# Differential-attention core scored two units ahead, stage loads issued earlier, and some copies moved to ScalarE

## Chip, cores and metric

The kernel runs on one core of a Trainium2 chip (trn2). The metric is device time in microseconds (us) of one execution, median of three runs. Engines: TensorE (PE, with its weight loads as PEld), VectorE (DVE), ScalarE (ACT), GpSimd (POOL); SyncE (SP) issues nearly all DMAs.

## What is computed

One encoder layer over 1024 positions of width 1024. One normalised input is projected into three branches (mLSTM, differential attention, retention) and three gates; the gated branch outputs are summed, projected, normed and added to x; a SwiGLU feed-forward follows. The part that matters most here:

```python
# 8 heads, 2 components of 64 per head, values of 128
for blk in range(S // Q_BLOCK):                  # 8 blocks of 128 queries
    kend = q0 + Q_BLOCK
    s = einsum('bqhcd,bkhcd->bhcqk', qb, kb)     # two score maps per head
    s = where(allowed, s - slope * dist, -inf)
    p = softmax(s, axis=-1)
    a = p[:, :, 0] - lam * p[:, :, 1]
    outs.append(einsum('bhqk,bkhe->bqhe', a, vb))
...
y = gm * (hm @ w_mlstm_out) + gd * (hd @ w_diff_out) + gr * (hr @ w_ret_out)
x = x + rmsnorm(y @ w_out);  x = x + rmsnorm((silu(a) * u) @ w_ffn_out)
```

## The kernel before, in words

Matmuls of full precision are made of three passes on a high and a low part of each operand (`mm3`, L111 to L113); `split_sbuf` (L105 on ACT, L106 on DVE) makes the two parts. The large products (input projection, feed-forward) use seven products in place of eight (`Seven`, `Unit`, `steady`); a unit has seven steps of 12 matmuls, and `follow` runs one step between two `yield`s.

Stages in order of time: `turned` transposes the normed x into seven operand roles (`L255` transposes, then ACT L265 makes the high part, DVE L266 a plain copy, DVE L267 the low part); `projections` runs the units while the mLSTM and retention cores are woven in; then `diff_core`, the differential attention; then the rest of the merge and `w_out` blocks with `norm_steps`; then `turned` again for the feed-forward; `feed_forward`; `down`.

`diff_core` runs 64 units (8 heads, and per head query blocks qb = 7 down to 0). Of a unit, `scores` makes two score maps (PE L850), adds the distance bias and takes the row maximum (DVE L852), negates it (L856) and takes the exponential with its row sum (ACT L857). `weights` combines the two maps (DVE L863, L865, L866). `turn` transposes the result (PE L876) and copies it (ACT or DVE L878). `values` multiplies with v (PE L886) and norms (ACT L213, DVE L890 and L207, POOL L208, DVE L894). `finish` transposes the output (PE L904). In the loop, while unit n is worked on, the scores of unit n+1 are issued after `turn` of n, and its `weights` in the second half.

`weave` runs other work between: each value that the core yields, times a rate, gives the number of steps of `dense` (the merge products of the mLSTM and retention branches, 12 matmuls a step, operands `bh`, `bl`, `wh`, `wl`) that are issued there. Tiles come from pools of fixed size: `big` (tag T, 32 tiles of 4 KB per partition), `half_tile` (tag s2k, 14 tiles of 2 KB), PSUM with 4 banks for dense work and 4 for the rest. A list scheduler then settles the order on each engine, and each engine and DMA queue runs its own list strictly in order.

In `diff_core` the loads of head 0 (`diff_load`, L809 and L810, `diff_load_v`, L814) are issued when the core starts. In `down`, `operands` loads one block of the hidden activations (L1230) and splits it just ahead of its products.

Of the kernel before, what the change touches and what calls it, by code (L numbers as in the profile page):

```python
# [8 lines left out]
F32 = mybir.dt.float32  # L9
# [3 lines left out]
ALU = mybir.AluOpType  # L13
# [27 lines left out]
def trunk(ctx: ExitStack, tc: tile.TileContext, x, norm_gains, w_in, mlstm_conv, mlstm_gate_bias,  # L41
# [18 lines left out]
    def big(shape, dtype=F32, name="t"):  # L60
        return pool.tile(shape, dtype, tag="T", bufs=N_T, name=nm(name))
# [187 lines left out]
    def turned(src, sh, g, seven, xs):  # L249


        for kt in range(KT) if sh == 0 else (4, 5, 0, 1, 6, 7, 2, 3):
            ps = psum()
            for i in range(4):
                nc.tensor.transpose(ps[:, i * P:(i + 1) * P], src[i][:, kt * P:(kt + 1) * P], ident)  # L255
            col = pcol[:, g + kt:g + kt + 1]
            role, q = "A" + str(sh + 1) + str(kt // 4 + 1), kt % 4
            if (role, q // 2) not in xs:
                xs[role, q // 2] = big([P, 2, HALF], name="hx")
            x = xs[role, q // 2][:, q % 2, :]  # L260
            if role == "A21":
                nc.scalar.activation(x, ps, AF.Copy, scale=col)
            else:
                h, l = seven.slot(role, q)
                nc.scalar.activation(h, ps, AF.Copy, scale=col)  # L265
                nc.vector.tensor_scalar(x, ps, col, None, op0=ALU.mult)  # L266
                nc.vector.tensor_sub(l, x, h.bitcast(F32))  # L267
            yield

    def left_sums(seven, xs):  # L270
# [548 lines left out]
        return slice((c % 4) * P, (c % 4 + 1) * P)  # L819

    def diff_core():
        ndist = big([P, S], name="ndist")
        nc.scalar.dma_start(ndist, c_dist)
        for sh in (1, 0):
            diff_load(0, sh, diff_qk[0])
        diff_load_v(0, diff_qk[0])

        def scores(u):
            hd, qb = u["hd"], u["qb"]
            d = diff_qk[hd]  # L830
            if qb < 4 and hd + 1 < DH:
                after = diff_qk[hd + 1]
                if qb == 3:
                    diff_load(hd + 1, 1, after)
                    diff_load_v(hd + 1, after)
                if qb == 1:
                    diff_load(hd + 1, 0, after)
# [70 lines left out]

        units = [dict(hd=hd, qb=qb) for hd in range(DH) for qb in reversed(range(NT))]
        scores(units[0])  # L910
        yield 6
        weights(units[0])
        for n, u in enumerate(units):
            after = units[n + 1] if n + 1 < len(units) else None
            turn(u)
            if after is not None:
                scores(after)
            if n > 0:
                finish(units[n - 1])
# [5 lines left out]
            if u["qb"] == 0:  # L925
                diff_qk[u["hd"]].clear()
            yield w
        finish(units[-1])

# [126 lines left out]
    def norm_steps(sh, i):  # L1056

        st = sh * 4 + i
        t = z[sh][i]
        xt = big([P, D], name="xr")  # L1060
        nc.sync.dma_start(xt, x[st * P:(st + 1) * P, :])
        rstd = norm_factor(t)
        yield
        nc.vector.scalar_tensor_tensor(t, t, rstd, gains[1], op0=ALU.mult, op1=ALU.mult)
        nc.vector.tensor_add(xt, xt, t)  # L1065
        nc.sync.dma_start(x2_dram[st * P:(st + 1) * P, :], xt)
        rstd = norm_factor(xt)
        yield
        nc.vector.tensor_scalar(t, xt, rstd, None, op0=ALU.mult)

    def out_blocks():
        acc = {}
# [112 lines left out]
        keep("S4", p, s[3])  # L1185
        first.h = second.h = None

    def feed_forward():
        keep_hidden(*ups[:2])
        for n, _ in enumerate(steady(ups[3:])):  # L1190
            if n % 14 == 6:
                keep_hidden(*ups[n // 7 + 2:n // 7 + 4])
        for r in ROLES:
            h2.drop(r)

    def down():


        gains[3] = gain(3)
        f = [None] * NT  # L1200
        w = []

# [22 lines left out]
            nc.vector.tensor_sub(b12, b21, b12)  # L1225
            return b12

        def operands(role_l, role_r, p):
            t = half_tile()
            nc.sync.dma_start(t, hid[role_l][p])  # L1230
            o = [parts_tile([P, HALF]) for _ in range(2)]
            split_sbuf(*o[0], t)
            split_sbuf(*o[1], right(role_r, p))
# [5 lines left out]
        def product(role_l, role_r, ps, more):  # L1239
            for p in range(NP):  # L1240
                if role_r == "B11":
                    load(p)
                o = operands(role_l, role_r, p)
                for j in range(4):
                    step(ps[j], o, j, p == 0, p == NP - 1, more)

# [15 lines left out]
        def x2_of(st):  # L1262
            xt = big([P, D], name="x2")
            nc.sync.dma_start(xt, x2_dram[st * P:(st + 1) * P, :])
            return xt

        f[:] = [big([P, D], name="f") for _ in range(NT)]
        px = [psum(True) for _ in range(4)]
        product("A11", "B11", px, False)
# [3 lines left out]
        product("S1", "T1", py, False)  # L1273
        for j in range(4):
            nc.scalar.copy(f[j + 4][:, halfs(1)], py[j])
        product("S2", "T2", px, True)
        for j in range(4):
            nc.scalar.copy(f[j][:, halfs(1)], px[j])
        product("S4", "B22", py, True)
        for j in range(4):  # L1280
            nc.vector.tensor_add(f[j][:, halfs(1)], py[j], f[j][:, halfs(1)])
        product("S3", "T3", px, True)
# [3 lines left out]
        product("A12", "B21", pz, False)  # L1286
        for j in range(4):
            nc.vector.tensor_add(f[j][:, halfs(0)], pz[j], f[j][:, halfs(0)])
        s2 = [small([P, 2], "s2", bufs=8) for _ in range(NT)]
        held = []  # L1290
        for p in range(NP):
            o = operands("A22", "T4", p)
# [50 lines left out]
    ups = [up(i, own=i == 2) for i in range(FB)]  # L1343
    units[2].own = True
    made = [0]

    def projections():

# [97 lines left out]
    feed_forward()  # L1446
    down()


# [48 lines left out]
```

## Time and profile before

| | |
|---|---|
| median of three runs | 2746.5 us (2746.33 to 2747.31) |
| profiled execution | 2744.93 us, of which the span 2743.1 us |
| PE busy | 2563.2 us (93%) |
| DVE busy | 1755.2 us (64%) |
| ACT busy | 1222.5 us (45%) |
| mean granted TensorE clock | 0.971 |

The span is the time from the first to the last instruction in the trace. Busy PE time is made of matmuls that overlap in a pipeline, so a busy PE may still run below its best pace; the granted clock says how fast it was allowed to run (1.00 is 2.4 GHz).

### The profile page before, as it was taken

Reading aid. Unit: us, or ns where it says so; the run is one execution under the profiler, and the core shown is the slowest. Engines: PE = TensorE matmul, PEld = TensorE weight load, DVE = VectorE, ACT = ScalarE, POOL = GpSimd, SP = SyncE. Lnnn points to the kernel's source line nnn. Section 1 sums busy time; section 2 is a strip of 40 time slices with the busy share of each in tenths; the row PEclk is TensorE's granted clock in tenths of the full one; section 3 lists DMA queues with packets and bytes.
Section 4 is the critical chain, followed back from the end, with each engine's and each line's share of the span. In section 5 each row is a group of like instructions: output and inputs, shape, how many; then the busy total and the mean of one; then the engine's idle time right before and its main releaser. Section 6 shows DMA issues by size and latency. Waiting matters only on the chain. (4 is left out here: it accounts for less than half of the span.)

```text
span 2743.1 us, 35302 instructions
## 1 busy us (share of the span) xinstructions
PE 2563.2 (93%) x12061; PEld 2083.4 (76%) x12061; DVE 1755.2 (64%) x3638; ACT 1222.5 (45%) x2480; POOL 262.5 (10%) x393
## 2 busy tenths in 40 slices
PE   6999999999999999999978869879998999998997
PEld 4778888888788888888766657667876888886885
DVE  7678877666666666565456666664368555654756
ACT  4554554454344444554434444442254333332544
POOL 3000000000000000000000001112123201110000
PEclk9999999999999999999989989989998999999999
DMA  3244445444545555443564456546433323337342
GB/s 118 87 134 123 138 123 155 132 139 124 153 127 158 160 151 159 131 130 101 160 165 117 131 143 175 147 131 207 146 108 96 122 86 111 101 99 266 104 135 87
DMA packets 402079, 368.93 MB, mean 134 GB/s; under 512 B 18957, under 2 KB 302046, under 8 KB 401898
## 3 DMA queue, kind: packets, MB, share of 16 engines
q1 hardware_dynamic: 399424, 364.45, 44.5%
q10 hardware_dynamic: 2474, 2.22, 0.3%
q8 instruction: 95, 1.56, 0.2%
q14 instruction: 86, 0.70, 0.1%
HBM read 249.92 MB, written 116.69 MB: 134 GB/s over the span
## 5 line engine op out<-in xcount | busy, mean ns | idle before, releaser
L105 ACT CAST wh<-ws 128x512 fp32r<-128x512 f32 (+1 forms) x622 | 385.0, 623 | 748.2 <-PE ps L112 546.0
L106 DVE TENSOR_TENSOR wl<-ws,wh 128x512 fp32r<-128x512 f32 (+1 forms) x622 | 454.4, 734 | 234.3 <-ACT wh L105 228.9
L302 DVE TENSOR_TENSOR ws<-ws,ws 128x512 f32<-128x512 f32 x216 | 148.8, 689 | 99.8 <-DMA ws<-in_w_in_dram 56.1
L111 PE MATMUL ps<-bh,wh 128*128 128x512 f32 x384 | 156.9, 416 | 9.9 <-ACT bh L105 6.5
L112 PE MATMUL ps<-bl,wh 128*128 128x512 f32 x384 | 155.5, 407 | 1.7 <-DVE bl L106 1.7
L113 PE MATMUL ps<-bh,wl 128*128 128x512 f32 x384 | 155.1, 406 | 0.0
L315 ACT COPY s2k<-ps 128x512 f32<-128x512 f32 x234 | 136.0, 582 | 17.8 <-PE ps L113 15.7
L111 PE MATMUL ps<-A11h,wh 128*128 128x512 f32 x312 | 127.8, 410 | 11.4 <-ACT wh L105 9.1
L111 PE MATMUL ps<-S1h,wh 128*128 128x512 f32 x312 | 127.1, 409 | 8.1 <-ACT S1h L105 7.5
L857 ACT ACTIVATE sb<-sb,nmx 128x896 f32<-128x896 f32 (+7 forms) x128 | 98.3, 769 | 69.6 <-DVE nmx L856 69.4
L111 PE MATMUL ps<-S2h,wh 128*128 128x512 f32 x312 | 125.8, 404 | 3.6 <-ACT s2k L315 3.6
L111 PE MATMUL ps<-wh,wh 128*128 128x512 f32 x308 | 118.3, 392 | 11.4 <-ACT wh L105 11.4
L113 PE MATMUL ps<-A11h,wl 128*128 128x512 f32 x312 | 125.9, 403 | 2.3 <-DVE wl L106 2.3
L112 PE MATMUL ps<-S1l,wh 128*128 128x512 f32 x312 | 125.7, 403 | 1.5 <-DVE S1l L106 1.5
L111 PE MATMUL ps<-S3h,wh 128*128 128x512 f32 x312 | 125.0, 401 | 0.7 <-ACT s2k L315 0.7
L112 PE MATMUL ps<-A11l,wh 128*128 128x512 f32 x312 | 125.6, 403 | 0.0
L111 PE MATMUL ps<-S4h,wh 128*128 128x512 f32 x312 | 125.5, 402 | 0.0
L113 PE MATMUL ps<-S1h,wl 128*128 128x512 f32 x312 | 125.2, 401 | 0.0
L112 PE MATMUL ps<-wl,wh 128*128 128x512 f32 x308 | 120.9, 393 | 4.3 <-DVE wl L106 4.3
L111 PE MATMUL ps<-A12h,wh 128*128 128x512 f32 x312 | 124.7, 400 | 0.1
L112 PE MATMUL ps<-S2l,wh 128*128 128x512 f32 x312 | 124.5, 400 | 0.1
L111 PE MATMUL ps<-A22h,wh 128*128 128x512 f32 x312 | 124.6, 399 | 0.0
(294 smaller groups left out, 6520.3 us busy)
## 6 DMA issues: line engine op xcount, KB each, us to landing
ws<-in_w_in_dram SPq DMA_DIRECT2D x112, 512.0 KB, 4.5
ws<-in_w_ffn_in_dram SPq DMA_DIRECT2D x44, 512.0 KB, 3.9
m_dram<-s2k SPq DMA_DIRECT2D x64, 256.0 KB, 2.1
ch<-m_dram SPq DMA_DIRECT2D x32, 512.0 KB, 6.0
r_dram<-s2k SPq DMA_DIRECT2D x64, 256.0 KB, 2.3
ch<-r_dram SPq DMA_DIRECT2D x32, 512.0 KB, 5.2
qk_dram<-s2k SPq DMA_DIRECT2D x64, 256.0 KB, 3.3
dk<-qk_dram SPq DMA_DIRECT2D x64, 256.0 KB, 5.1
```

Of the source, the lines that this page charges most:

```text
L105: nc.scalar.copy(hi, src)
L106: nc.vector.tensor_sub(lo, src, hi.bitcast(F32))
L111: nc.tensor.matmul(ps, lh, rh, start=start, stop=False, skip_group_check=more)
L112: nc.tensor.matmul(ps, lh, rl, start=False, stop=False, skip_group_check=more)
L113: nc.tensor.matmul(ps, ll, rh, start=False, stop=stop, skip_group_check=more)
L302: self.eng.tensor_tensor(*sub[r], op=ALU.subtract)
L315: nc.scalar.copy(t, ps)
L857: nc.scalar.activation(sb[c], sb[c], AF.Exp, bias=nmx, scale=slope, accum_out=sm[:, c:c + 1])
```

## The change

Six edits. (1) In `turned`, for odd tiles, the low part is made straight from PSUM by one DVE operation, and the plain copy is made on ACT. (2) `diff_core` scores unit n+2 while unit n is worked on; the first two units are scored ahead with a larger yield, and score tiles of at most 512 columns come from the s2k pool. (3) The loads of the next head are issued at qb 4 and 3, those of head 0 in the last part of `projections`. (4) The last scaling in `norm_steps` goes from DVE to ACT. (5) `down` becomes a generator: its first loads and its first split are issued inside the last unit of `feed_forward`, and it keeps up to three hidden blocks loaded ahead. (6) The weave rate of the core is 63/892 instead of 64/832.

```diff
@@ turned
-                nc.vector.tensor_scalar(x, ps, col, None, op0=ALU.mult)
-                nc.vector.tensor_sub(l, x, h.bitcast(F32))
+                if kt % 2:
+                    nc.vector.scalar_tensor_tensor(l, ps, col, h.bitcast(F32), op0=ALU.mult, op1=ALU.subtract)
+                    nc.scalar.activation(x, ps, AF.Copy, scale=col)
+                else:
+                    nc.vector.tensor_scalar(x, ps, col, None, op0=ALU.mult)
+                    nc.vector.tensor_sub(l, x, h.bitcast(F32))
@@ diff_core
-            sb = u["sb"] = [big([P, kend], name="sb") for _ in range(2)]
+            sb = u["sb"] = [big([P, kend], name="sb") if kend > HALF else half_tile([P, kend]) for _ in range(2)]
...
         scores(units[0])
-        yield 6
+        yield 20
+        scores(units[1])
         weights(units[0])
+        yield 40
         for n, u in enumerate(units):
-            after = units[n + 1] if n + 1 < len(units) else None
+            hd, qb = u["hd"], u["qb"]
+            later = units[n + 2] if n + 2 < len(units) else None
+            if hd + 1 < DH:
+                if qb == 4:
+                    diff_load(hd + 1, 1, diff_qk[hd + 1])
+                if qb == 3:
+                    diff_load(hd + 1, 0, diff_qk[hd + 1])
+                    diff_load_v(hd + 1, diff_qk[hd + 1])
             turn(u)
-            if after is not None:
-                scores(after)
+            if later is not None:
+                scores(later)
             if n > 0:
                 finish(units[n - 1])
-            w = (after["qb"] if after is not None else 0) + 3
+            w = qb + 3
             yield w
-            if after is not None:
-                weights(after)
+            if n + 1 < len(units):
+                weights(units[n + 1])
             values(u)
@@ norm_steps
-        nc.vector.tensor_scalar(t, xt, rstd, None, op0=ALU.mult)
+        nc.scalar.activation(t, xt, AF.Copy, scale=rstd)
@@ feed_forward
+        last = 7 * (FB - 3)
         for n, _ in enumerate(steady(ups[3:])):
+            if n in (last - 8, last - 3):
+                next(second)
@@ down
+        def operands():
+            k = done[0]
+            make(k + 1)
+            load_left(k + 4)
+            done[0] += 1
+            o, ready[k] = ready[k], None
             return o
+        load_left(3)
+        yield
+        make(1)
+        yield
@@ projections
+            if i == n - 8:
+                dist.append(big([P, S], name="ndist"))
+                nc.scalar.dma_start(dist[0], c_dist)
+                diff_load(0, 1, diff_qk[0])
+            if i == n - 6:
+                diff_load(0, 0, diff_qk[0])
+                diff_load_v(0, diff_qk[0])
@@ end
-    weave(diff_core(), 64 / 832)
+    weave(diff_core(), 63 / 892)
```

Three places show what this does to the order on the engines. **Inside the core**, PE before: `sb_3214` is the unit qb = 3 of head 1, scored into `ps_3218` and `ps_3220`.

```order
L876 MATMUL ps_3206_13994<-ident_66,sb_3187_13929 128x128 x4
L850 MATMUL ps_3218_14020<-dk_3065_13543,dq_3064_13542 128x512
L850 MATMUL ps_3220_14027<-dk_3065_13543,dq_3064_13542 128x512
L904 MATMUL ps_3222_14034<-ident_66,hk_3205_13978 128x128
L886 MATMUL ps_3225_14042<-dv_3023_13428,s2k_3207_13999 128x128 x4
L111 MATMUL ps_3378_14502<-bh_2986_13313,wh_3235_14077 128x512
L876 MATMUL ps_3238_14083<-ident_66,sb_3214_14016 128x128 x4
```

PE after, same head: `sb_3173` is the unit qb = 4, scored into `ps_3177` (and three more), turned two score sets later.

```order
L843 MATMUL ps_3177_13908<-dk_3060_13572,dq_3028_13484 128x512
L879 MATMUL ps_3194_13964<-dv_3062_13580,s2k_3170_13896 128x128 x4
L869 MATMUL ps_3200_13996<-ident_66,sb_3150_13823 128x128 x4
L843 MATMUL ps_3208_14012<-dk_3060_13572,dq_3059_13571 128x512
L897 MATMUL ps_3212_14026<-ident_66,hk_3199_13980 128x128
L879 MATMUL ps_3215_14034<-dv_3062_13580,s2k_3201_14001 128x128 x4
L112 MATMUL ps_3222_14053<-bl_2924_13120,wh_3054_13561 128x512
L869 MATMUL ps_3226_14075<-ident_66,sb_3173_13904 128x128 x4
```

DVE after, same stretch: the weights of `sb_3173` (its last row is L859) stand ahead of the copy for the unit being turned (L871) and of the next unit's bias row.

```order
L849 TENSOR_SCALAR nmx_3182_13927<-mx_3175_13906 128x1
L883 TENSOR_SCALAR ds_3196_13973<-ds_3196_13973,rec_3161_13867 128x1
L207 TENSOR_SCALAR dv_3198_13977<-ds_3196_13973 128x1
L887 TENSOR_SCALAR hk_3199_13980<-ps_3194_13964,dfac_3197_13976,rec_3161_13867 128x128
L856 RECIPROCAL rec_3213_14029<-sm_3176_13907 128x2
L858 TENSOR_SCALAR rat_3214_14031<-rec_3213_14029,sm_3176_13907,neg_lam_90 128x1
L859 SCALAR_TENSOR_TENSOR sb_3173_13904<-sb_3174_13905,rat_3214_14031,sb_3173_13904 128x640
L1023 TENSOR_TENSOR s2k_3185_13934<-ps_3186_13936,s2k_3185_13934 128x512
L871 COPY s2k_3203_14006<-ps_3202_14003 128x256
L845 ISA s2k_3204_14008,mx_3206_14010<-ps_3208_14012,ndist_2862_12873 128x512
```

Before, one output transposition, one product with v and dense rows lay between a unit's scores and its own turn. After, a whole further unit lies there as well: a product, a turn, a score set, an output transposition and a product. Dense rows stay between product and turn in both.

**At the start of the core**, SP after. `branch0` rows are the operands of the dense steps, `dk`, `dq`, `dv` the loads of head 0.

```order
L462 DMA gate1_76<-s2k_2859_12865 128x512
L813 DMA dk_2874_12925<-qk_dram_81 64x2x512 x2
L814 DMA dq_2873_12924<-qk_dram_81 64x2x512
L813 DMA dk_2875_12926<-qk_dram_81 64x2x512
L462 DMA gate1_76<-s2k_2867_12897 128x512
L818 DMA dv_2876_12933<-dv_dram_82 128x8x128
L994 DMA s2k_2882_12969<-branch0_72 128x512
L994 DMA s2k_2885_12975<-branch0_72 128x512
L994 DMA s2k_2886_12994<-branch0_72 128x512
```

Before, all eight `branch0` loads and four weight loads (L148) stood ahead of the first `dk` load; now the second half of head 0 stands ahead of the first `branch0` load, and the first half further up still.

**At the start of `down`**, SP before: the first reads of hidden blocks (L1230) follow the four sums that the last pair of units stores.

```order
L1168 DMA hid_S1_94<-s2k_5419_22751 128x512
L1168 DMA hid_S3_96<-s2k_5421_22753 128x512
L1168 DMA hid_S2_95<-s2k_5420_22752 128x512
L1168 DMA hid_S4_97<-s2k_5422_22754 128x512
L1230 DMA s2k_5438_22781<-hid_A11_91 128x512
L1230 DMA s2k_5445_22807<-hid_A11_91 128x512
```

SP after: three reads stand ahead of those stores, the fourth (`s2k_5451`) behind them.

```order
L1243 DMA s2k_5408_22637<-hid_A11_91 128x512
L1243 DMA s2k_5411_22643<-hid_A11_91 128x512
L1243 DMA s2k_5414_22649<-hid_A11_91 128x512
L1170 DMA hid_S1_94<-s2k_5432_22777 128x512
L1170 DMA hid_S3_96<-s2k_5434_22779 128x512
L1170 DMA hid_S2_95<-s2k_5433_22778 128x512
L1170 DMA hid_S4_97<-s2k_5435_22780 128x512
L1243 DMA s2k_5451_22807<-hid_A11_91 128x512
```

So three of the eleven blocks of the first product can be in place before the last pair is stored.

## Rows read from the trace of the kernel before

**Rows 1.** Busy time by stretch: start:end, length, engines with counts, clock, DMA share.

```profile
core 0: us, PE busy (x) PEld busy (x) DVE busy (x) ACT busy (x) POOL busy (x), PEclk, DMA share, GB/s
1368.00:1390.00 22.00, 5.00 (x15) 3.45 (x15) 4.57 (x13) 2.54 (x5) 0.00 (x0) 0.63 0.73 167
1390.00:1852.00 462.00, 391.09 (x2038) 315.66 (x2037) 302.94 (x1003) 206.91 (x563) 57.17 (x78) 0.93 0.53 143
2040.00:2100.00 60.00, 46.08 (x181) 34.85 (x180) 49.52 (x54) 31.98 (x51) 23.79 (x15) 0.83 0.25 79
2400.00:2450.00 50.00, 50.00 (x216) 40.27 (x215) 27.89 (x40) 18.46 (x32) 5.56 (x4) 1.00 0.32 103
```

**Rows 2.** Waits of PE, 1390 to 1852: waiter, releaser, total us, times, longest.

```profile
PE ps L876 <- DVE sb L866: 31.6, 18, 6.4
PE ps L876 <- DVE dv L207: 24.6, 12, 2.8
PE ps L111 <- ACT bh L105: 5.1, 3, 2.2
```

**Rows 3.** Timeline of one unit (qb = 4): start, length, engine, line, operation, idle before.

```profile
1582.91 2.76 PE L850 MATMUL ps<-dk,dq 128*128 128x512 f32 x8
1585.64 1.50 PE L886 MATMUL ps<-dv,s2k 128*128 128x128 f32 x12
...
1587.06 0.81 ACT L857 ACTIVATE sb<-sb,nmx 128x640 f32<-128x640 f32 x1
1588.57 0.88 DVE L866 SCALAR_TENSOR_TENSOR sb<-sb,rat,sb 128x640 f32<-128x640 f32 x1
1589.59 0.74 PE L876 MATMUL ps<-ident,sb 128*128 128x128 f32 x5 [2.45 <-DVE dv L207]
```

**Rows 4.** Waits of DVE, 1390 to 1852.

```profile
DVE rec L863 <- ACT sb L857: 48.6, 47, 1.9
DVE hk L894 <- POOL dfac L208: 36.3, 53, 1.0
DVE ds L890 <- ACT junk L213: 34.2, 19, 3.8
```

**Rows 5.** Timeline of PE, and of the load queue SP, where the core starts.

```profile
1365.82 6.40 SPq L809 DMA_DIRECT2D dk<-qk_dram  x2
1377.54 2.90 PE L850 MATMUL ps<-dk,dq 128*128 128x512 f32 x6 [9.46 <-DMA dk<-qk_dram]
...
1388.68 1.97 PE L876 MATMUL ps<-ident,sb 128*128 128x128 f32 x8 [6.82 <-DVE sb L866]
```

**Rows 6.** Timeline where `down` starts: SP, ACT, PE.

```profile
2501.94 4.62 SPq L1168 DMA_DIRECT2D hid_S<-s2k  x4
2506.61 3.29 SPq L1230 DMA_DIRECT2D s2k<-hid_A  x7
2509.35 0.62 ACT L105 CAST wh<-s2k 128x512 fp32r<-128x512 f32 x1 [9.55 <-DMA s2k<-hid_A]
2510.54 0.79 PE L111 MATMUL ps<-wh,wh 128*128 128x512 f32 x1 [11.43 <-ACT wh L105]
```

**Rows 7.** Groups by line, 2000 to 2100, DVE and ACT: busy us, mean ns.

```profile
L266 DVE TENSOR_SCALAR hx<-ps,pcol 128x512 f32<-128x512 f32 x12 | 8.4, 745 | 4.0 <-PE ps L255 2.2 <-ACT A22h L265 1.2 <-ACT A11h L265 0.6
L1065 DVE TENSOR_TENSOR xr<-xr,z 128x1024 f32<-128x1024 f32 x5 | 6.1, 1222 | 0.2
L1069 DVE TENSOR_SCALAR z<-xr,xr 128x1024 f32<-128x1024 f32 x8 | 6.0, 752 | 3.4 <-POOL xr L208 3.3
L213 ACT ACTIVATE junk<-xr 128x1024 bf16<-128x1024 f32 x6 | 6.3, 1057 | 10.7 <-DVE xr L1065 10.6
```

**Rows 8.** Timeline of PE: the first turn of heads 2, 3 and 4.

```profile
1509.14 1.03 PE L876 MATMUL ps<-ident,sb 128*128 128x128 f32 x8
1565.37 1.03 PE L876 MATMUL ps<-ident,sb 128*128 128x128 f32 x8
1630.85 1.09 PE L876 MATMUL ps<-ident,sb 128*128 128x128 f32 x8 [0.59 <-DVE sb L866]
```

More of the change, by code (lines that the diff above doesn't have):

```diff
@@ L821, in diff_core @@
     def diff_core():
[L822 to L826, printed above, removed]
+        ndist = dist[0]
         def scores(u):
@@ L830, in scores @@
             d = diff_qk[hd]
[L831 to L837, printed above, removed]
             slope = 2.0 ** (-8.0 * (hd + 1) / DH)
@@ L1186, in keep_hidden, with feed_forward @@
         first.h = second.h = None
-    def feed_forward():
+    def feed_forward(second):
         keep_hidden(*ups[:2])
+        last = 7 * (FB - 3)
         for n, _ in enumerate(steady(ups[3:])):
+            if n in (last - 8, last - 3):
+                next(second)
             if n % 14 == 6:
@@ L1196, in down @@
     def down():
-        gains[3] = gain(3)
         f = [None] * NT
@@ L1226, in right, with load_left, make, product @@
             return b12
[L1228 to L1233, printed above, removed]
-            return o
+        order = [(l, r, p) for l, r in (("A11", "B11"), ("S1", "T1"), ("S2", "T2"), ("S4", "B22"), ("S3", "T3"),
+                                        ("A12", "B21"), ("A22", "T4")) for p in range(NP)]
+        left, ready = [], []
+        def load_left(n):
+            while len(left) < min(n, len(order)):
+                role_l, role_r, p = order[len(left)]
+                if role_r == "B11":
+                    load(p)
+                t = half_tile()
+                nc.sync.dma_start(t, hid[role_l][p])
+                left.append(t)
+        def make(n):
+            while len(ready) < min(n, len(order)):
+                k = len(ready)
+                _, role_r, p = order[k]
+                load_left(k + 1)
+                o = [parts_tile([P, HALF]) for _ in range(2)]
+                split_sbuf(*o[0], left[k])
+                split_sbuf(*o[1], right(role_r, p))
+                left[k] = None
+                ready.append(o)
+        done = [0]
+        def operands():
[4 more added lines that the diff above has]
+            o, ready[k] = ready[k], None
+            return o
+        load_left(3)
+        yield
+        make(1)
+        yield
         def step(ps, o, j, first, last, more):
             mm3(ps, cols_at(o[0], j * P, (j + 1) * P), o[1], first and not more, last, more)
-        def product(role_l, role_r, ps, more):
+        def product(ps, more):
             for p in range(NP):
-                if role_r == "B11":
-                    load(p)
-                o = operands(role_l, role_r, p)
+                o = operands()
                 for j in range(4):
@@ L1265, in x2_of @@
             return xt
+        gains[3] = gain(3)
         f[:] = [big([P, D], name="f") for _ in range(NT)]
         px = [psum(True) for _ in range(4)]
-        product("A11", "B11", px, False)
+        product(px, False)
         for j in range(4):
@@ L1272, in down @@
         py = [psum() for _ in range(4)]
-        product("S1", "T1", py, False)
+        product(py, False)
         for j in range(4):
             nc.scalar.copy(f[j + 4][:, halfs(1)], py[j])
-        product("S2", "T2", px, True)
+        product(px, True)
         for j in range(4):
             nc.scalar.copy(f[j][:, halfs(1)], px[j])
-        product("S4", "B22", py, True)
+        product(py, True)
         for j in range(4):
             nc.vector.tensor_add(f[j][:, halfs(1)], py[j], f[j][:, halfs(1)])
-        product("S3", "T3", px, True)
+        product(px, True)
         for j in range(4):
@@ L1285, in down @@
         pz = [psum() for _ in range(4)]
-        product("A12", "B21", pz, False)
+        product(pz, False)
         for j in range(4):
@@ L1291, in down @@
         for p in range(NP):
-            o = operands("A22", "T4", p)
+            o = operands()
             if p < NP - 4:
@@ L1345, in trunk @@
     made = [0]
+    dist = []
     def projections():
@@ L1445, in trunk @@
     z[1][:] = [None] * 4
-    feed_forward()
-    down()
+    second = down()
+    feed_forward(second)
+    for _ in second:
+        pass
 _INS = ["x", "norm_gains", "w_in", "mlstm_conv", "mlstm_gate_bias", "diff_lambda", "diff_subln",
```

4 lines of the change are left out of this document (2 added, 2 removed).

## The prediction

> **What bounds the kernel now.** I read the busy time by stretch first, then the waits of PE in the stretches where it isn't full, then the timeline there. In a full stretch PE starts 216 matmuls in 50 us at clock 1.00, 0.231 us each [rows 1]. Most of the span looks like that, and PE is the bound there; nothing in this change touches it. Time can only come from the stretches where PE stands still or runs slowly. There are four: the start of the differential core, the core itself, the second call of `turned`, and the start of `down`.
>
> In the core, 1390 to 1852, PE is busy 391.1 of 462 us at a clock of 0.93 [rows 1], so 71 us are idle, and of the busy time 0.07 x 391.1 = 27 us go to the lower clock. The waits name nearly one cause: `turn` (L876) waits 31.6 + 24.6 = 56.2 us, 30 times [rows 2]. The second row names L207, but what L876 reads is the combined map of L866; in the timeline of one unit L866 ends at 1589.45 and the turn starts at 1589.59, 6.68 us after its scores started [rows 3]. So the whole chain scores, maximum, two exponentials, weights, turn is waited for.
>
> **The change, part by part.**
>
> *Start of the core (3).* PE waits 9.46 us for `dk` and 6.82 us for the first weights [rows 5], and its 5.0 us of work run at clock 0.63 [rows 1]: 16.3 + 1.8 = 18 us. The first loads were late because their second half waited 6.4 us on SP [rows 5]. Now they stand ahead of the last stores, and four dense steps lie between the first scores and the first turn (48 matmuls, 11.1 us at 0.231) with a second score set, against a wait of 6.82: covered. What is late next are the operands of those dense steps, since their loads now stand behind those of head 0 on SP. One such wait costs up to 2.2 us [rows 2]. The gain lies between 7 (only the second wait goes, the first becomes a wait for `bh`) and 18; I take 15, near the upper end, since the loads move some twenty microseconds up.
>
> *Two units ahead (2, 6).* Between the scores of a unit and its turn PE had 6.68 - 2.45 = 4.2 us of work of its own [rows 3]. A further unit adds the same again and a turn, some 9 us, against a chain of 6.7. The margin of 2.5 us is spent on DVE: the weights now stand in DVE's list behind the norm of an earlier unit, which itself waits for POOL (36.3 us over 53 times) and for ACT (34.2 us) [rows 4], and ahead of the copy that the unit being turned needs. Both ends: none of the 56.2 us is left, or DVE's own waits take the place of three quarters of them and 15 are gained. I take two thirds, 37.5 us, as the margin is positive but thin in the small units, where a unit is short and the chain is mostly fixed latencies.
>
> Of the 27 us at the lower clock a part comes back. The clock fell where PE had stood still: 0.63 in the stretch with 17 idle of 22 us, 0.93 with 71 idle of 462, 1.00 in the full one [rows 1]. With two thirds of the main wait gone I take half, 13.5 us; the ends are 0 and 27.
>
> A check from DVE: busy 302.9 us, and with the waits for POOL and ACT in the norm 373 us; with its wait for the exponentials (48.6 us [rows 4]) 422. The core after, 462 - 51 = 411 us, lies between. DVE stays just short of being the bound.
>
> *Score tiles from the s2k pool.* No instruction is added. Three units in flight take at most six of 14 tiles, their transposes two, the output one, dense work two to four: eleven to thirteen. Priced at nothing while that holds; the rival below prices the other case.
>
> *Loads of the next head (3)* are issued at qb 4 and 3 and needed at qb 1, two units later, as before. Nothing.
>
> *Start of `down` (5).* PE waits 11.43 us [rows 6]. Its last matmul was over at 2510.54 - 11.43 = 2499.1. Three blocks can now be ready: 36 matmuls, 8.3 us, to 2507.4. The fourth read still stands behind the four stores of sums on SP, so it is issued at 2506.61; its first landing came 2.74 us later and the matmul 1.19 us after that [rows 6]. PE then waits from 2507.4 to 2510.5. Gain 8.3, I take 8; ends 5 (a block less) and 11.4.
>
> *`turned` and `norm_steps` (1, 4).* Twelve tiles in two calls lose one DVE operation of two, 0.745 us each, and the low part stays one operation; the eight norm tiles lose 0.752 us each [rows 7]: 15 us off DVE. ACT takes the twelve copies and the eight scalings; its nearest row is 1.057 us for 1024 columns [rows 7]. In 2040 to 2100 DVE is busy 49.5 us of 60, ACT 32.0, and PE does 181 matmuls, 41.9 us at full pace, 18 us lost [rows 1]. There fall two of the tiles and about four of the scalings, 4.5 us of DVE time. I take 3 us; the ends are -2 (each of the last four scalings on the path, 0.3 us later, and an order that happens worse) and 8 (the first call gains as well).
>
> The scaling that is moved was DVE's quick one: 0.752 us for 1024 columns, where the addition next to it takes 1.222 [rows 7]. The Trainium skill (VectorE: DVE Perf Modes, "The perf-mode tier table (the rule you actually need)") says why: a float32 operation with one tensor input from SBUF runs at twice the rate of one with two tensor inputs. The trace agrees, 0.752 against 1.222. By that rule this edit moves work from the faster engine to the slower, and if the four late scalings lie on the path, the term would be 1.8 instead of 3, and the time 1 us more.
>
> **Sum.** 15 + 37.5 + 13.5 + 8 + 3 = 77 us. The profiled execution took 2744.9 us, 1.6 below the median of the runs; 2744.9 - 77 + 1.6 = 2669.5, say 2670. The low ends together (7 + 15 + 0 + 5 - 2 = 25) give 2721, the high ends (18 + 56 + 27 + 11 + 8 = 120) 2626.
>
> **The rivals.**
>
> *DVE takes over as the bound.* The weights of the next unit stand ahead of the copy for the unit being turned, so `values` waits for DVE where `turn` did before. For it: DVE is at 66% in the core, its in-order waits already make 119 us in three rows [rows 4], and PE would have to run at nearly its own floor. Against it: the wait for the exponentials should shrink, since they were begun a unit earlier. Price: the core stays at 422 us, and the copy is late by half of a weights row (0.88 us [rows 3]) in 63 units, 28 us, less what dense work covers, say 15: a gain of 25 in the core, 51 in all, 2695; 2686 to 2716 as its range.
>
> *PE reaches its floor.* All of L876's waits go and the clock stays up: 391.1 - 27 = 364 us, plus 15 us of other waits, 379 in the core. 15 + 83 + 8 + 3 = 109 us, 2637. Against it: DVE's 373 us would be as long, and two queues that run in order don't overlap without loss.
>
> *The distance isn't used.* The scheduler may pull the weights forward until DVE works at the old distance, and only start and `down` gain: 23 us, less some order lost, 2725 to 2745. The order inside the core speaks against it.
>
> *Slower: the s2k pool runs dry.* The four small units of each head hold six tiles of s2k, and if the gate and branch loads of dense work wait for a tile, SP stops behind them and PE has no dense steps to fill with. A head in which that work was short shows the price: head 3 took 65.5 us where head 2 took 56.2 [rows 8], 9.3 us. The head would also lose its share of the gain, 51 / 8 = 6.4. Each such head costs 15.7 us, so from five heads on (77 / 15.7 = 4.9) the change loses; with all eight it is 2669 + 126 = 2795. Against it: the count above stays at or under 13 of 14, and the order shows dense rows in the small units.
>
> **How the numbers follow.** Chances: forecast 0.49 (2650 to 2686), DVE bound 0.27, PE floor 0.12 (2626 to 2650), distance not used 0.06, pool 0.06. The range 2636 to 2716 holds the forecast, nine tenths of the second case and about half of the third, 0.79. A measurement of this kernel can tell about 0.2%, 5.5 us, from no change. Faster by more: the first three and half of the fourth, 0.91; within: the other half, 0.03; slower: 0.06.
>
> **What would show it.** The stretch from the last projection matmul to the first turn, 20 us and mostly idle now, becomes some 15 us with PE full; if PE waits there for `bh`, the first term was too large. L876's wait falls from 56 us to 15 to 20, and the core from 462 us to about 411 with the clock at 0.96 or more. If L879 waits for the copy instead, or DVE's waits before its norm rows grow, the first rival holds. If the core is long while PE waits before dense rows and SP waits for tiles, the last. At the start of `down` one wait of about 3 us is left, before the fourth block. PE in the stretch around the second `turned` does some ten more matmuls in 60 us. A stretch of plain `steady` that isn't as full as before would make the whole sum wrong: early loads that hold up the weights.

## The result, and the profile after

The changed kernel takes 2660.0 us (median of four runs, 2657.3 to 2660.6), against 2746.9 for the kernel before on the same chip: a ratio of 0.968, interval [0.966, 0.970]. That is 87 us faster; 77 were forecast, and 2670 us. The time lies in the range, the direction and the main mechanism were right, and the terms were not the right size: two were too small, one was a little too large, one had the wrong sign.

The profiled execution has a span of 2655.5 us (before 2743.1), so 87.6 us are to be accounted for. I cut both traces at the same five places of PE's work, to within half a microsecond: the last matmul of the projections (after the change the first scores follow it at once; before, dense rows and the wait for the loads did), the last output transposition of the core, the last dense product, the last product of the feed-forward's main part, the end. Busy time by stretch, the kernel before (start:end, length, then each engine's busy time with its count, clock, DMA share, GB/s): the core, the feed-forward with the second `turned` ahead of it, `down`.

```profile
1355.40:1855.70 500.30, 410.04 (x2108) 328.97 (x2106) 312.42 (x1026) 214.84 (x578) 57.72 (x79) 0.92 0.55 146
1945.30:2498.30 553.00, 536.17 (x2296) 430.71 (x2295) 338.28 (x458) 209.81 (x355) 97.03 (x69) 0.98 0.35 116
2498.30:2743.10 244.80, 213.88 (x928) 173.98 (x926) 154.88 (x257) 104.81 (x199) 11.32 (x12) 0.96 0.43 141
```

The same three stretches after the change, and behind them the core without its start.

```profile
1355.20:1769.50 414.30, 381.65 (x2106) 307.69 (x2106) 301.35 (x1028) 212.23 (x582) 60.21 (x80) 0.98 0.64 172
1857.50:2416.70 559.20, 536.70 (x2295) 430.79 (x2295) 331.73 (x447) 224.27 (x373) 96.12 (x69) 0.98 0.35 116
2416.70:2655.50 238.80, 214.98 (x928) 175.08 (x927) 155.28 (x254) 102.45 (x195) 11.70 (x12) 0.96 0.43 141
...
1377.00:1770.00 393.00, 362.05 (x2028) 292.32 (x2026) 286.69 (x993) 199.02 (x560) 60.21 (x80) 0.99 0.63 166
```

The core is 86.0 us shorter and does the same matmuls (2106 and 2108). Of the 86.0, idle time gave 57.6 (500.3 - 410.0 = 90.3, now 414.3 - 381.7 = 32.7), and 28.4 came out of PE's busy time, where the clock rose from 0.92 to 0.98. The stretch with the second `turned` became 6.2 us longer, all of it idle (16.8 to 22.5) but for half a microsecond. `down` became 6.0 us shorter. Between core and feed-forward 1.6 were gained, and 0.2 ahead of the core: 87.6.

The waits of PE in the core after (waiter, releaser, total us, times, longest) answer to [rows 2]:

```profile
PE ps L111 <- ACT bh L105: 7.1, 4, 3.8
PE ps L897 <- DVE hk L887: 7.0, 7, 2.1
PE ps L843 <- DVE hk L887: 5.6, 11, 0.9
PE ps L897 <- DVE nmx L849: 4.9, 8, 1.1
PE ps L869 <- DVE dv L207: 2.4, 2, 1.9
PE ps L869 <- DVE s2k L859: 1.7, 2, 1.0
```

L869 is the turn (L876 before). Its 56.2 us are 4.1 now. Cut as the prediction cut it, from the first turn to the last, the core took 385.0 us (1377 to 1762) where 411 were forecast and 462 were there before. What is late next are the output transposition (L897, 11.9 us; in the core before it waited 3.1 for the normed output) and scores that stand behind the norm of an earlier unit (L843, 5.6). The waits of DVE answer to [rows 4]:

```profile
DVE hk L887 <- POOL dfac L208: 29.9, 49, 1.9
DVE ds L883 <- ACT junk L213: 13.4, 17, 3.7
...
DVE rec L856 <- ACT s2k L850: 12.0, 14, 1.5
...
DVE rec L856 <- ACT sb L850: 5.0, 6, 1.4
```

The wait for the exponentials fell from 48.6 to 17.0 us, and the two waits inside the norm from 70.5 to 43.3.

At the start of the core the timeline of PE is full but for 1.40 us and, just behind, 0.22 us. Before, it stood 9.46 and 6.82 us [rows 5], and 0.72 us between the two, which [rows 5] leaves out. The row of that third wait before, then three rows after:

```profile
1381.16 0.70 PE L850 MATMUL ps<-dk,dq 128*128 128x512 f32 x2 [0.72 <-DMA dk<-qk_dram]
```

```profile
1355.26 1.99 PE L843 MATMUL ps<-dk,dq 128*128 128x512 f32 x8
...
1362.84 0.50 PE L111 MATMUL ps<-bh,wh 128*128 128x512 f32 x1 [1.40 <-ACT bh L105]
...
1376.20 1.03 PE L869 MATMUL ps<-ident,sb 128*128 128x128 f32 x8
```

At the start of `down` the queue SP still puts the fourth read behind the four sums, and PE waits there once, before the fourth block; in [rows 6] it was 11.43 us before the first.

```profile
2420.75 4.96 SPq L1170 DMA_DIRECT2D hid_S<-s2k  x4
2425.80 1.83 SPq L1243 DMA_DIRECT2D s2k<-hid_A  x4
...
2429.79 2.07 PE L111 MATMUL ps<-wh,wh 128*128 128x512 f32 x4 [4.01 <-ACT wh L105]
```

Around the second `turned` the transposes (L255) wait for the scaling that ACT now does. The group of the transposes before, with 8.5 us of waits; then, after the change, the same group with 12.8 and the group of the scaling; then three rows of the timeline after:

```profile
L255 PE MATMUL ps<-ident,z 128*128 128x128 f32 x64 | 12.4, 344 | 8.5 <-DVE z L1069 3.3 <-DVE xv L207 2.8 <-DVE s2k L1151 1.3
```

```profile
L255 PE MATMUL ps<-ident,z 128*128 128x128 f32 x64 | 11.3, 316 | 12.8 <-ACT z L1071 8.6 <-DVE hx L270 1.8 <-DVE s2k L1153 1.7
L1071 ACT ACTIVATE z<-xr,xr 128x1024 f32<-128x1024 f32 x8 | 9.1, 1143 | 5.7 <-POOL xr L208 5.7
```

```profile
1974.84 0.55 POOL L208 TENSOR_TENSOR xr<-xv,expo 128x1 f32<-128x1 f32 x1 [4.56 <-DVE xv L207]
1975.42 1.15 ACT L1071 ACTIVATE z<-xr,xr 128x1024 f32<-128x1024 f32 x1 [0.85 <-POOL xr L208]
...
1976.62 1.11 PE L255 MATMUL ps<-ident,z 128*128 128x128 f32 x4 [3.82 <-ACT z L1071]
```

The factor comes from POOL, ACT scales for 1.15 us, and PE starts at the end of it, after the longest of these waits. On DVE the same scaling took 0.752 us [rows 7].

### The profile page after: what moved, and what is told of

Same layout as the page of the kernel before. It is cut to its first block, busy times and chain, and to the rows that moved or that the text cites. A ratio compares the mean times of both kernels' runs of the same rounds, so it can differ in the third digit from the quotient of the medians.

```text
span 2655.5 us, 35304 instructions
## 1 busy us (share of the span) xinstructions
PE 2534.3 (95%) x12061; PEld 2062.1 (78%) x12061; DVE 1731.7 (65%) x3618; ACT 1233.6 (46%) x2500; POOL 262.8 (10%) x393
## 5 line engine op out<-in xcount | busy, mean ns | idle before, releaser
L111 PE MATMUL ps<-A11h,wh 128*128 128x512 f32 x312 | 127.7, 409 | 14.6 <-ACT wh L105 12.6
L459 DVE TENSOR_TENSOR s2k<-ps,s2k 128x512 f32<-128x512 f32 x108 | 74.3, 688 | 78.7 <-PE ps L113 70.8
L112 PE MATMUL ps<-S4l,wh 128*128 128x512 f32 x312 | 124.1, 398 | 0.0
```

Source lines behind the costliest of these rows:

```text
L111: nc.tensor.matmul(ps, lh, rh, start=start, stop=False, skip_group_check=more)
L112: nc.tensor.matmul(ps, lh, rl, start=False, stop=False, skip_group_check=more)
L459: nc.vector.tensor_add(part, ps, part)
```

## The experiments

Each kernel is the changed one with the edit shown. All twelve are compared with runs of the kernel before on their own chip; the medians of before there were 2746.7 to 2749.2 us, so the ratios compare better than the times.

| kernel | median us | ratio to before, interval |
|---|---|---|
| the change | 2660.0 | 0.968 [0.966, 0.970] |
| scores one ahead | 2711.7 | 0.987 [0.986, 0.989] |
| head 0 loaded late | 2669.1 | 0.972 [0.970, 0.973] |
| norm scaling on DVE | 2654.3 | 0.966 [0.965, 0.968] |
| `turned` as before | 2656.5 | 0.967 [0.966, 0.969] |
| `down` not begun early | 2667.1 | 0.971 [0.969, 0.973] |
| core alone | 2673.9 | 0.974 [0.972, 0.976] |
| both copy edits undone, five blocks ahead | 2655.0 | 0.967 [0.965, 0.968] |
| the same, output transposition later | 2647.1 | 0.964 [0.962, 0.966] |
| all score tiles in T | 2683.8 | 0.977 [0.975, 0.979] |
| small first yields | 2657.3 | 0.967 [0.966, 0.968] |
| scores three ahead | 2645.8 | 0.963 [0.961, 0.964] |
| norm scaling on DVE, transposition later | 2644.6 | 0.963 [0.961, 0.964] |

**Scores one ahead.** My theory is that the distance of two makes most of the gain. The rival is that the new order, the pool and the rate make it, and the distance little.

```diff
-        scores(units[1])
...
-            later = units[n + 2] if n + 2 < len(units) else None
+            later = units[n + 1] if n + 1 < len(units) else None
```

> The changed kernel with one edit taken back: scores one unit ahead instead of two (the early loads, the pools of the score tiles, the larger first yields and the rate stay). Theory (the distance between a unit's scores and its turn is what took the 56.2 us of waits away, and the clock follows): the waits of the turn come back to 40 to 55 us, the clock in the core falls to 0.95 or less, and the time rises from 2660 to 2715 to 2730. Rival (what helped are the score tiles in the other pool, the loads and the dense steps at the start): the waits of the turn stay under 15 us and the time within 10 us of 2660.

It took 2711.7 us, 51.7 more than the change. Waits of PE in its core, and its busy time there:

```profile
PE ps L869 <- DVE sb L859: 20.0, 10, 4.9
PE ps L869 <- DVE dv L207: 17.0, 12, 2.5
PE ps L869 <- DVE s2k L859: 2.1, 4, 1.1
```

```profile
1354.80:1820.40 465.60, 398.83 (x2106) 317.90 (x2104) 310.41 (x1028) 215.28 (x581) 59.71 (x79) 0.96 0.57 152
```

The turn waits 39.1 us again, the clock is 0.96, and the core is 51.3 us longer: 34.1 of them idle, 17.2 in the busy time of as many matmuls. Wait, clock and time all stop a little short of what was expected. The distance is the main cause, and it acts twice, through the wait and through the clock. Of the 52.1 us that the turn's wait had lost, two thirds came back (35.0), so the other edits have a share in it too, some 17 us that the distance alone doesn't explain. And 4.8 us of this run's idle time are one wait for a late load of dense work, not a wait of the turn.

**Head 0 loaded late.** The loads of head 0 stand at the start of the core again.

```diff
+        ndist = big([P, S], name="ndist")
+        nc.scalar.dma_start(ndist, c_dist)
+        for sh in (1, 0):
+            diff_load(0, sh, diff_qk[0])
+        diff_load_v(0, diff_qk[0])
...
-            if i == n - 8:
-                dist.append(big([P, S], name="ndist"))
-                nc.scalar.dma_start(dist[0], c_dist)
-                diff_load(0, 1, diff_qk[0])
-            if i == n - 6:
-                diff_load(0, 0, diff_qk[0])
-                diff_load_v(0, diff_qk[0])
```

> The changed kernel with the loads of head 0 and of the distance table issued when the core starts, as before. Theory (they must stand ahead of the core's first matmul, or PE waits for them): PE waits 8 to 10 us for the first loads again, and the time rises by 8 to 11 us to 2668 to 2671. Rival (dense steps cover the loads, since four of them are now issued around the first scores): no change beyond 3 us.

2669.1 us, 9 more. In PE's timeline the old wait is back, a little shorter than the 9.46 us of before:

```profile
1371.19 2.90 PE L847 MATMUL ps<-dk,dq 128*128 128x512 f32 x6 [8.32 <-DMA dk<-qk_dram]
```

```profile
1350.70:1780.70 430.00, 389.31 (x2107) 310.94 (x2106) 301.43 (x1026) 210.23 (x579) 59.92 (x80) 0.96 0.65 171
```

By the totals the earlier loads are worth 9 us. The second row is the core of this run, and it is 15.7 us longer than the change's (430.0 and 414.3): 8.0 of them idle, 7.7 in PE's busy time. So these loads, too, act through the clock. The profiled executions differ by 12.6 us in all and the medians by 9: in this one the projections ended 4.5 us earlier, which lies within the spread that the last section shows.

**Small first yields.** The rest of that term should be the cover of the first chain by dense steps.

```diff
-        yield 20
+        yield 6
...
-        yield 40
+        yield 6
...
-    weave(diff_core(), 63 / 892)
+    weave(diff_core(), 63 / 844)
```

> The change with 6 and 6 in place of the two larger first yields (20 and 40), and the rate of the weave set so that as many dense steps are woven in all: hardly any dense work is handed out between the first scores and the first turn. Theory: those steps cover the first chain of scores, maximum, exponential and weights, so PE waits 4 to 7 us before the first turn again and the time is 2664 to 2668. Rival: the scheduler fills the gap with dense rows anyway, and the time stays within 3 us of 2660.

2657.3 us; the rival holds. The scheduler still sets 47 dense matmuls between the first scores and the first turn, in place of 58, and the first turn doesn't wait. So the larger yields don't make the cover. Two other runs show what does: with the scores one ahead there is no second score set before the first turn, only 56 dense matmuls, and with head 0 loaded late a second score set and only 7. The first turn doesn't wait in either, so each of the two is enough there; no run takes both away.

**Norm scaling on DVE.** The stretch around the second `turned` lost time. Theory: the scaling on ACT is the cause.

```diff
-        nc.scalar.activation(t, xt, AF.Copy, scale=rstd)
+        nc.vector.tensor_scalar(t, xt, rstd, None, op0=ALU.mult)
```

> The changed kernel with the last scaling in the norm back on DVE. Theory (ScalarE takes 1.14 us for it where DVE took 0.75, and it waits in ScalarE's list behind other rows, on the path to the transposes): the waits of the transposes for z, 8.6 us, fall to 3 to 5, and the time falls by 2 to 5 us to 2655 to 2658. Rival (DVE is the busier engine there and needs the relief): the time rises by 1 to 4 us.

2654.3 us. The intervals of the two ratios overlap, so the total alone doesn't decide; the stretch does. It is 553.7 us long in place of 559.2, with nearly the idle time of before (17.8 us). The row of that stretch, and the groups of the scaling and of the transposes:

```profile
1856.80:2410.50 553.70, 535.92 (x2296) 430.58 (x2295) 337.24 (x455) 216.00 (x365) 95.89 (x69) 0.98 0.35 117
```

```profile
L1071 DVE TENSOR_SCALAR z<-xr,xr 128x1024 f32<-128x1024 f32 x8 | 6.0, 753 | 3.4 <-POOL xr L208 3.3
L255 PE MATMUL ps<-ident,z 128*128 128x128 f32 x64 | 12.0, 332 | 9.0 <-DVE z L1071 3.6 <-DVE xv L207 3.0 <-DVE hx L270 1.2
```

The waits of the transposes fall from 12.8 to 9.0 us. Those put down to the scaling fall from 8.6 to 3.6, but 3.0 are now put down to L207, a row of the norm whose result the transposes don't read, as in the kernel before (2.8); counted with them it is 6.6. The edit also reaches where it wasn't aimed: the core of this kernel takes 417.9 us, 3.6 more than the change's, with one wait of an output transposition of 5.3 us that the change doesn't have. So the 6 us of the total are not the stretch alone.

**`turned` as before.** The other copy edit undone.

```diff
-                if kt % 2:
+                if False:
```

> The changed kernel with the plain copy of odd tiles back on DVE in both calls of the transposing stage. Theory (the odd tile's PSUM bank is now read three times in a row, by ScalarE, DVE and ScalarE, so it comes free 0.7 us later, and the plain copy that the sums need is late): the time falls by 1 to 4 us to 2656 to 2659. Rival (DVE relief is worth what was predicted): the time rises by 1 to 3 us.

2656.5 us by the median, which is what the theory said, but the intervals overlap. The stretch of the second `turned` takes 559.5 us against the change's 559.2, and the transposes still wait 8.4 us for the scaling. No difference is shown: this edit is worth nothing that can be told here.

**`down` not begun early.**

```diff
-            if n in (last - 8, last - 3):
-                next(second)
```

> The changed kernel with the first loads and the first split of the last stage issued only after the feed-forward loop (the reads three blocks ahead stay). Theory (the first product waited because its reads stood behind the stores of the last sums in SP's list): the wait before the first product is 11 us again in place of 4.0 before the fourth block, and the time rises by 6 to 8 us to 2666 to 2668. Rival (the scheduler moves the reads up anyway): within 2 us of 2660.

2667.1 us, 7 more. PE waits before the first block again:

```profile
2431.61 0.80 PE L111 MATMUL ps<-wh,wh 128*128 128x512 f32 x1 [11.28 <-ACT wh L105]
```

**Core alone.** All but the core's own order, pools and rate undone: late loads of head 0, both copy edits, and `down` as before, with one block loaded at a time (`load_left(k + 1)`, no `load_left(3)`, no `make(1)`).

> The kernel before with the core's edits alone: two units ahead, score tiles in the other pool, loads of the next head, first yields and rate. Loads of head 0, the transposing stage, the norm and the last stage as before. Theory (the parts add): 2660 + 9 (late loads) - 6 (norm) + 7 (last stage) and -3 to 0 for the transposing stage: 2667 to 2671, so about 77 of the 87 us are the core's own. Rival (the parts need each other): 2680 or more.

2673.9 us, 3 above the expected stretch. The core alone is worth 73 of the 87 us.

**Both copy edits undone, five hidden blocks ahead.** With the 4 us left at `down` as the aim:

```diff
-        load_left(3)
+        load_left(5)
```

> The changed kernel with the two copy edits (transposing stage and norm) taken back and five in place of three hidden blocks read ahead at the start of the last stage. Theory: 6 us from the norm, 0 to 3 from the transposing stage, and the 4.0 us wait before the fourth block goes: 2646 to 2651. Rival (reading five blocks early holds tiles or SP that the last feed-forward unit needs): 2654 or more.

2655.0 us, as much as with the norm scaling alone, so the rival's time came. From the last dense product to the end the two kernels take 793.0 and 792.5 us. The wait didn't go, it moved from the fourth block to the first:

```profile
2411.78 0.73 PE L111 MATMUL ps<-wh,wh 128*128 128x512 f32 x2 [3.87 <-ACT wh L105]
```

**Output transposition later.** The largest wait left in the core is that of `finish`; here, on top of the last kernel, it is issued behind the dense steps of its unit.

```diff
-            if n > 0:
-                finish(units[n - 1])
             w = qb + 3
             yield w
+            if n > 0:
+                finish(units[n - 1])
```

> The kernel of the run before, with the output transposition of a unit issued after the dense steps of the next unit's first half in place of ahead of them. Theory (the 12 us that PE waits before these transpositions, 7.0 for the normed output and 4.9 put down to the row after it on DVE, are a distance that is too short): the waits fall under 4 us and the time by 5 to 10 us. Rival (DVE's list sets the pace by now, and a wait only moves to the next row that DVE serves): no change beyond 3 us.

2647.1 us, 7.9 less than the last kernel on the same chip. The wait of L897 fell from 16.2 us to 8.7 (8.4 + 7.8 to 5.1 + 3.6), less far than expected; the time came out as forecast.

**All score tiles in T.** What is the smaller pool for the small score tiles worth?

```diff
-            sb = u["sb"] = [big([P, kend], name="sb") if kend > HALF else half_tile([P, kend]) for _ in range(2)]
+            sb = u["sb"] = [big([P, kend], name="sb") for _ in range(2)]
```

> The change with all score tiles in the pool of large tiles T, none in s2k. Theory: the move of the small score tiles is needed by the distance of two: with three units of a head in flight up to six of the large tiles are taken, the operands of the next head and the dense work wait for free tiles, and PE waits for loads: slower than the change by 5 to 20 us, 2665 to 2680. Rival: the large pool has tiles to spare, and the time stays within 3 us of 2660.

2683.8 us, 24 more than the change: the theory's direction, above its size. Busy time and waits of PE in its core:

```profile
1354.50:1792.90 438.40, 389.80 (x2106) 310.66 (x2105) 302.12 (x1028) 211.55 (x581) 60.45 (x80) 0.98 0.60 162
```

```profile
PE ps L843 <- DVE hk L887: 11.5, 15, 2.2
PE ps L843 <- DMA dq<-qk_dram: 4.3, 1, 4.3
PE ps L869 <- DVE sb L859: 4.0, 2, 3.5
PE ps L869 <- DVE rec L856: 4.0, 2, 2.1
```

The core is 24.1 us longer: 15.9 idle, 8.2 in PE's busy time. One load of `dq` comes late, 4.3 us. In all its rows the turn waits 10.1 us instead of 4.1, and the scores behind the norm (L843) 11.5 instead of 5.6. Which tile was waited for, the trace doesn't say; that late loads are the cause, as the theory had it, is shown for 4.3 of the 24 us only, and the rest is open. Whether the pool is worth as much at one ahead was not run.

**Scores three ahead.**

```diff
+        scores(units[2])
...
-            later = units[n + 2] if n + 2 < len(units) else None
+            later = units[n + 3] if n + 3 < len(units) else None
```

> The change with the scores three units ahead in place of two. Theory: the wait of PE before the turn is already down to 4 us, so a further unit has nothing left to hide; within 5 us of 2660, or slower where the four small units hold eight of the s2k tiles. Rival: the first units of each head still lose time through the chain, and a third unit takes off 5 us or more: 2655 or less.

2645.8 us, 14 less than the change: my theory fell, the rival holds. Busy time and waits of PE in its core:

```profile
1352.20:1752.70 400.50, 377.86 (x2099) 302.14 (x2098) 300.12 (x1027) 211.30 (x580) 60.75 (x80) 1.00 0.66 177
```

```profile
PE ps L897 <- DVE hk L887: 7.7, 12, 1.7
PE ps L897 <- DVE nmx L849: 4.8, 7, 1.1
PE ps L843 <- DVE hk L887: 2.9, 6, 1.1
PE ps L111 <- ACT bh L105: 2.0, 2, 1.2
```

The core is 13.8 us shorter: 10 of idle time (32.7 to 22.6) and 3.8 of busy time. The turn doesn't wait at all; its 4.1 us went, and with them 5.1 of the waits for `bh` and 2.7 of the scores behind the norm. The wait of the transposition didn't shrink (11.9 us to 12.5 in these rows). So the third unit doesn't only hide the chain that the second was meant to hide. That the scheduler has more rows to choose from may be the reason; no run shows it.

**Norm scaling on DVE and the later transposition together.**

```diff
-        nc.scalar.activation(t, xt, AF.Copy, scale=rstd)
+        nc.vector.tensor_scalar(t, xt, rstd, None, op0=ALU.mult)
...
-            if n > 0:
-                finish(units[n - 1])
             w = qb + 3
             yield w
+            if n > 0:
+                finish(units[n - 1])
```

> The change with the norm scaling back on DVE (worth 6 us by itself) and the output transposition of the core issued behind the dense steps of the unit (worth 8 us by itself on another version). Theory: the two are in different stretches and add up: 2644 to 2649. Rival: the later transposition only moves its wait to the product with v, and the time is not under 2652.

2644.6 us, level with three ahead and the best; the two stretches add up as the theory says. Its core took 406.7 us, 7.6 less than the change's, the stretch of the second `turned` 555.1. This kernel with three units ahead was not run.

## Why the prediction was right, and where not

| term | forecast us | in the traces us | |
|---|---|---|---|
| start of the core | 15 | 15.4 | idle time alone, 17.0 to 1.6 |
| two ahead, idle time | 37.5 | 42.2 | 57.6 less the start's 15.4 |
| two ahead, clock | 13.5 | 28.4 | busy time of the core's matmuls, the start's among them |
| start of `down` | 8 | 6.0 | 7 by its own run |
| `turned` and `norm_steps` | 3 | -6.2 | idle time |
| ahead of and behind the core | 0 | 1.8 | |
| sum | 77 | 87.6 | |

The total is nearer than the terms, and that is luck in part: the two terms of two ahead were put 20 us too low together, `down` and the last term 11 us too high.

**Start.** The size was right, and the loads' part is shown by undoing them (8.3 us of waiting for `dk`, 15.7 in the core with the clock). The cover of the first turn was there as well, 58 dense matmuls and a second score set. That these dense rows need the larger yields, from which the prediction counted its four steps, was wrong: the scheduler draws dense rows there without them. The prediction named a wait for `bh` as what is late next, up to 2.2 us; it was 1.4.

**Two ahead.** The mechanism was right and the size wrong. I took two thirds of the 56.2 us, since DVE's in-order list would hold the weights back; nine tenths of the turn's wait went. That list didn't hold them back: begun a unit earlier, the exponentials were mostly done when DVE asked for them (48.6 to 17.0 us), and even the norm's waits shrank, which I had taken as fixed at 70.5. Part of the turn's gain came back as waits of the output transposition and of the scores, so the idle time fell by 42.2 and not by 52. Three ahead shows that two don't use the distance up; the experiment's theory, that nothing was left to hide, took the turn's wait for all that distance can hide.

**The clock.** The other step that failed: "with two thirds of the main wait gone I take half". Half was too little. At one ahead the idle time of the core is 66.8 us (465.6 - 398.8) and the clock 0.96; at two 32.7 and 0.98, at three 22.6 and 1.00. PE's busy time falls with it, 410.0, 398.8, 381.7, 377.9 us for as many matmuls (2099 to 2108). So the clock comes back faster than the idle time goes, and about as fast as the turn's wait: of the 32.8 us worked out below, one ahead gives back a third (11.2) with three tenths of that wait gone (56.2 to 39.1), two ahead nearly nine tenths with nine tenths gone. By the clocks of the two core rows, 0.08 of 410.0 and 0.02 of 381.7, 32.8 us were lost before and 7.6 after: 25 of the 28.4. The clock is printed to a hundredth, which is 2 us either way in each row, so the rest is within the reading. Not all of this is the distance's: taking the distance back costs 17.2 us of busy time, loading head 0 late 7.7.

**`down`.** The step was right in kind and 2 us too large: three blocks ready, the fourth late behind the four sums. PE waited 4.0 us there, not 3. Five blocks ahead don't remove it, since the first block then comes late.

**`turned` and `norm_steps`.** The sign was wrong. The step that failed is "I take 3 us", with -2 as its lower end: it priced the scalings by DVE's busy share. DVE did get 6.6 us of that stretch back (338.3 to 331.7), but DVE was not what PE waited for. The scaling is the last link of a chain statistic, power on POOL, scaling, transpose, and the link became 0.39 us longer (1.143 for 0.752); the prediction had put 0.3, from ACT's 1.057. The transposes wait for it four times in the trace, so 1.6 us come from the longer link itself, and even eight times would be 3.1, less than the 5.5 that the run with the scaling on DVE gave back. ACT also does the statistic of the next tile (1.05 us) in the same queue, so the scaling can delay that as well; this part is argued, no run separates it.

For the engine's price the Trainium skill had it (ScalarE: Activation LUTs, "What ACT_TABLE_LOAD costs"): 186 ns and 0.833 ns a column, and some 93 ns more for a scale that is read from memory. For 1024 columns that gives 1132 ns, an estimate; the trace agrees, 1143.

**The rivals.** DVE as the bound fell: DVE is busy 286.7 of 393 us and waits less than before (107 us in all its rows of the core, 151 before). PE's floor came nearest: it had the clock up and 15 us of waits left in the core. Two ahead has 0.98 and 32.7 us idle; three ahead, with 1.00 and 22.6, nearly reaches it. That the distance isn't used fell with the run at one ahead. A dry s2k pool fell even at three ahead. But the pool counts the other way round: the prediction put the move to it at nothing, and with the small tiles in T 24 of the 87 us are lost.

## What to carry to other kernels

A wait of PE that is spread over many units cost twice here: the idle time, and the lower clock of the work around it. Price both, and when the distance of a look-ahead is raised, try one step more, even when the wait it was meant for is nearly gone, since other waits can shrink with it. Before an operation is moved from a busy engine to an idle one, look whether it stands at the end of a chain: then its duration counts, not only the engine's share.

## What had not been expected of the hardware

A stretch in which nothing was changed can differ by 5 us between executions. In the fourteen traces of this document, whose kernels differ little up to there, the last matmul of the projections starts between 1350.2 and 1356.0 us, with early loads and without. The kernel with the norm scaling on DVE has the same order on PE up to the core as the change, yet its core starts at 1350.4 us, not 1355.3. A part of that shows early, 50 to 100 us after the start. The change, and then the other kernel:

```profile
50.00:100.00 50.00, 43.32 (x170) 33.65 (x169) 40.78 (x43) 23.63 (x34) 15.62 (x11) 0.86 0.22 63
```

```profile
50.00:100.00 50.00, 43.78 (x181) 33.94 (x180) 43.52 (x47) 24.46 (x36) 16.33 (x13) 0.93 0.24 68
```

As long a busy time, eleven matmuls more, at a clock of 0.93 instead of 0.86. The loss of 2.5 us that eleven matmuls make (at 0.231 us) is half of the 4.9. So gains of a few microseconds were read here by stretch, not by the total.

DVE's price depends on where the operand lies. It scales 512 columns from PSUM in 0.746 us (L270 in the second `turned`) and 1024 columns from SBUF in 0.752: twice the columns in the same time. ACT takes 0.690 us for 512 columns from PSUM (L268) and 1.143 for 1024 from SBUF. So the two engines are level for the one copy and far apart for the other. Whether the place counts for ACT as well, these rows don't show, as the number of columns differs too.
